# A hybrid encoder layer on one core: two single-half up-projection jobs instead of three, x split by token groups, and norm sums by a matrix of ones

## The chip, the cores and the metric

The kernel runs on one core of a Trainium2 chip. The metric is the device time of one execution in microseconds (us), shown as the median of several runs. TensorE (PE, with its weight loads PEld), VectorE (DVE), ScalarE (ACT), GpSimd (POOL) and the DMA queue of SyncE (SP) each work through a list of their own and wait for each other by semaphores.

## What is computed

One layer of an encoder trunk for 1024 prompt frames and 64 sample frames of width 1024. The two groups are laid side by side as 1088 columns (tokens) of eight tiles of 128 rows (features), and they share all weights. The reference, cut to its skeleton:

```python
mem_k, mem_v = rms_norm(mem) @ xk_w, rms_norm(mem) @ xv_w        # 256 memory tokens, prompt only
h = rms_norm(x, norm_mix_g)
q, fl, iv, og, ca, cg, pu = split(h @ w_in)
mix = [HGRN2(q, fl, iv, og), conv31(ca * sigmoid(cg)), pooling(pu)]
x = x + concat(mix) @ w_out
x = x + cross_attention(rms_norm(x, norm_x_g), mem_k, mem_v)      # 4 heads
h = rms_norm(x, norm_ffn_g)
x = x + square(relu(h @ w_up)) @ w_down                           # 1024 -> 4096 -> 1024
y = rms_norm(x, final_g)
```

rms_norm divides each token by the root of the mean of its squares over the 1024 features, and multiplies by a gain per feature. Besides y, the states, the caches and the memory keys and values are outputs.

## The kernel before

All operands of the large products are kept as a high and a low part (hi, lo; for weights wh, wl), each rounded to a format that TensorE takes at one column per step, and a product is three matmuls: hi by hi, lo by hi, hi by lo (`mm3`). The high part is a copy by ACT (`act`, line 126), the low part is what is left, by DVE (`split_lo`, line 138, or a scalar_tensor_tensor, line 141, where a gain is applied too). Weights arrive as raw blocks of 128x1024 (tile wr), `prep` (line 166) splits one into wh and wl; three split blocks fit in the pool, four raw ones. Working tiles come from a pool of 35 slots, results of products from 2 x 4 banks of 512 columns, tagged d (psd) and m (psm). Where the program does not fix the order by `inorder`, a scheduler places the instructions of each engine.

The stages, in order of time:

**Memory** (`memory`, line 290). Eight blocks of wk make the keys, and meanwhile x is loaded and its squares are summed. Then eight steps k (lines 362 to 378) multiply the memory by the blocks of wv: a step is 12 matmuls of 512 columns. After step 1 the norm of x is computed (`rstd_cols` and `bcast_rows`), and from step 2 on each step also issues, for one of the eight tiles of x, `scale_x` (x times the norm, DVE, 1088 columns) and `normed` (hi by ACT, then lo by DVE, which waits for hi). The last two tiles follow behind the loop.

**Mixers** (`mixers`, line 432). The input projection is 18 blocks of 128 columns, each a `dense` (line 212): three groups of tokens (364, 364, 360), and in each group eight tiles k by three matmuls. The first block goes across: for each k all three groups, so that it can begin when only the first tiles of x are split. Its four first blocks make the gated input of the convolution (csig, a sigmoid by ACT, and glu, a product by DVE). Later heads, convolution and pooling run beside the products.

**Attention** (line 785). The norm comes from `rstd_rows`: for nine tiles of 128 tokens a product of the squares (as the stationary operand) by one column of ones, then root (ACT) and reciprocal (DVE) on 9 columns, then a product with the identity for each of the nine tiles to spread the values over all rows, then copies by ACT into the tile rb.

**Up projection** (`mlp`, line 1109, and `up`, line 1061). It is a Strassen-like scheme: the tokens are cut into two halves c = 0 and 1 of 544, and each half gets seven operands "1" to "7" (th, tl), made by sums and splits of quarters (`operands`, line 967; its steps are called a for half 0, b for half 1). The 32 output blocks are 16 pairs; the weights of a pair are summed (`pair_sums`, 4 sums of 128x512) and split (`pair_units`, eight parts of 128x512). A job is one pair for one or for both halves: seven products in the order 1562734, each 12 matmuls of 272 columns and half. With LATE = 3 the jobs are: pairs 0 to 2 for half 0, pairs 3 to 15 for both halves, pairs 0 to 2 for half 1, 19 in all. In a job of one half the sums run on DVE, else on POOL. The steps of half 1 are spread over the first jobs by the lists handed to `up` (lines 1154 to 1157): its norm (rbb, from `rstd_half`, line 956), its operands (b), and at the end the loads and splits of the first results for the down projection (t_load, sp) and of the residual (xr_load).

**Down projection and end** (lines 1160 to 1227). Results are read back by blocks of four, split, multiplied and added to xr. The last block runs by three groups of tokens of 416, 416 and 256; behind each group its norm is computed (line 1206), POOL multiplies the first two groups by it, and DVE and POOL share the third.

Of the kernel before, what the change touches and what calls it, by code (L numbers as in the profile page):

```python
# [4 lines left out]
F32 = mybir.dt.float32  # L5
F32R = mybir.dt.float32r
U8 = mybir.dt.uint8
AF = mybir.ActivationFunctionType
# [3 lines left out]
P = 128  # L12
# [27 lines left out]
LATE = 3  # L40
# [12 lines left out]
class Trunk:  # L53
# [201 lines left out]
    def rstd_rows(self, sqs, dim, tag="m"):  # L255
        return self.bcast_rows(self.rstd_cols(sqs, TT, dim, tag), tag)

    def bcast_rows(self, r, tag="m"):
        rb = self.slot(n="rb")
        for (t0, m), tts, c0 in zip(SEGS, (TT[0:4], TT[4:8], TT[8:9]), (0, 4, 8)):  # L260
            ps = self.bank(tag)
            self.bcast_cols(ps, r, tts, t0, c0)
            self.act(rb[:, t0:t0 + m], ps[:, :m], AF.Copy)
        return rb
# [25 lines left out]
    def memory(self):  # L290
# [71 lines left out]
        for k in range(KT):  # L362
            wh, wl = self.weights()
            wh = wh.rearrange("p k n -> p (k n)")
            wl = wl.rearrange("p k n -> p (k n)")
            for m in range(2):
                for n in range(2):
                    sl = slice(512 * n, 512 * n + 512)
                    self.mm3_t(banks[m][n], xs[k][0][:, m * P:m * P + P], xs[k][1][:, m * P:m * P + P], wh[:, sl],
                               wl[:, sl], k == 0, k == KT - 1)  # L370
            if k == X_COLS:
                r_x = self.rstd_cols([accs[1]], TT, D, "d")
            elif k == X_ROWS:
                rx = self.bcast_rows(r_x, "d")
                self.act(self.warm, self.eps, AF.Sigmoid)
            if k >= X_ROWS:
                self.scale_x(k - X_ROWS, rx)
                hs.append(self.normed(k - X_ROWS))
# [5 lines left out]
        for j in range(KT - X_ROWS, KT):  # L384
            self.scale_x(j, rx)
            hs.append(self.normed(j))
# [16 lines left out]
    def scale_x(self, k, rb):  # L403
        x = self.xraw[k][:, :T]
        self.tt(x, x, rb[:, :T], MUL)

    def normed(self, k):
        x = self.xraw[k][:, :T]
        return self.hl(x, self.vec("mix_g", k))
# [22 lines left out]
    def mixers(self, xs):  # L432
# [10 lines left out]
        first = True  # L443

        glus = []
        for c in range(2):
            sig = self.slot(n="csig")
            self.dense(self.weights(), xs, ks, plain(sig, AF.Sigmoid), across=first)
            first = False
            glu = self.slot(n="glu")  # L450
            nc.gpsimd.memset(glu[:, 0:HIST], 0.0)
            nc.scalar.dma_start(glu[:, HIST + TP:2 * HIST + TP], a["cconv"][:, c, :])

            def ev(b, t0, m):
# [4 lines left out]
            self.dense(self.weights(), xs, ks, ev)  # L459
            nc.scalar.dma_start(a["o_convp"][c * P:c * P + P, :], glu[:, TP:TP + HIST])  # L460
            nc.scalar.dma_start(a["o_convs"][c * P:c * P + P, :], glu[:, HIST + T:HIST + T + HIST])
            glus.append(glu)
# [493 lines left out]
    def rstd_half(self, c):  # L956
        r = self.rstd_cols([self.accs[c]], CT, D, "m")
        yield
        for tts, c0 in ((CT[:4], 0), (CT[4:], 4)):
            ps = self.bank("m")  # L960
            t0, m = tts[0][0], sum(x[1] for x in tts)
            self.bcast_cols(ps, r, tts, t0, c0)
            self.act(self.rb[:, c, t0:t0 + m], ps[:, :m], AF.Copy)
        yield
# [144 lines left out]
    def mlp(self, o, x1, x2src):  # L1109
# [38 lines left out]
        def xr_load():  # L1148
# [7 lines left out]
            NPAIR: [lambda: t_load(f0)], NPAIR + 1: [sp, xr_load, sp, xr_load, sp, xr_load, sp],  # L1156
            NPAIR + 2: [xr_load] * 5})
# [32 lines left out]
        for g in ((0, 416), (416, 416), (832, 256)):  # L1190
# [14 lines left out]
            tts = [(c, min(P, m - c)) for c in range(0, m, P)]  # L1205
            r = self.rstd_cols([acc, sq] if last else [acc], tts, D)
            ps = self.bank("m")
            self.bcast_cols(ps, r, tts, 0)
            self.act(acc[:, :m], ps[:, :m], AF.Copy)
# [182 lines left out]
```

## Time and profile before

| what | value |
|---|---|
| time, median of 3 runs | 1566.14 us (1560.39 to 1567.87) |
| the profiled execution, its own time | 1564.72 us |
| its span, first to last instruction | 1562.9 us |
| DVE busy | 902.6 us (58%) |
| ACT busy | 587.5 us (38%) |
| POOL busy | 123.2 us (8%) |
| granted TensorE clock, mean | 0.993 |

Spans and stages below are of the profiled execution; times are counted from its first instruction. A busy time of PE contains modelled ends of pipelined matmuls that overlap; what PE really lost in a stretch is read from the number of matmuls in it (x...), against the number in an undisturbed stretch of the same length.

### The profile page before, as it was taken

What the parts mean: (1) busy time and instruction counts of PE and PEld (TensorE: products, weight loads), DVE (VectorE), ACT (ScalarE), POOL (GpSimd) and SP (SyncE); (2) the same over time, 40 slices, a digit from 0 to 9 for tenths busy, and PEclk for the clock granted to TensorE, in tenths of its full rate; (3) what the DMA queues carried; (4) which work ended last, traced back from release to release, by engine and by line L of the source; (5) the groups of instructions that cost most, each with busy time, mean ns of one, the idle gap of its engine ahead of it and who ended that gap; (6) DMA issues with size and microseconds to landing.
All of it is one profiled execution on the core that took longest, in us unless ns stands there. A gap on an engine that the chain in (4) does not pass through costs nothing.

```text
span 1562.9 us, 24283 instructions
## 1 busy us (share of the span) xinstructions
PE 1532.2 (98%) x10204; PEld 1486.5 (95%) x10204; DVE 902.6 (58%) x1329; ACT 587.5 (38%) x1072; POOL 123.2 (8%) x101
## 2 busy tenths in 40 slices
PE   8999999999999999999998999999999999999997
PEld 7799898999999999989998999999999999999997
DVE  7638988375654433684579545555585444434434
ACT  7422213556372222463555344444463111111133
POOL 0100001200000000000001222222100000000005
PEclk9999999999999999999999999999999999999999
DMA  9421011010013311223532233232286223211003
GB/s 347 137 83 55 15 41 32 18 41 18 31 66 145 127 55 55 68 78 113 184 113 97 98 112 112 98 112 85 98 320 241 99 100 109 94 59 53 29 1 115
DMA packets 54941, 150.58 MB, mean 96 GB/s; under 512 B 6704, under 2 KB 14384, under 8 KB 54832
## 3 DMA queue, kind: packets, MB, share of 16 engines
q1 hardware_dynamic: 51952, 148.37, 27.3%
q8 instruction: 80, 1.31, 0.3%
q10 hardware_dynamic: 2880, 0.66, 0.2%
q14 instruction: 29, 0.24, 0.0%
HBM read 115.11 MB, written 33.91 MB: 95 GB/s over the span
## 4 chain that ended last, share of the span: by engine, by line
PE 85%; issue 6%; DVE 4%; ACT 2%; POOL 1%; DMA 1%; SPq 0%; POOLq 0%; ACTq 0%; DVEq 0%
PE psd L210 66%; PE psm L210 13%; PE psm L560 3%; POOL xr L137 1%; DVE wl L138 1%; ACT hi L126 1%; PE psm L638 1%; DVE x L138 1%; PE psm L612 0%; PE psm L640 0%; PE psm L542 0%; DMA t<-tt 0%; PE psd L881 0%; DMA wr<-wk 0%; ACT L126 0%
## 5 line engine op out<-in xcount | busy, mean ns | idle before, releaser
L210 PE MATMUL psd<-hi,wl 128*128 128x364 f32 (+3 forms) x1536 | 507.0, 330 | 0.3 <-DVE wl L138 0.3
L210 PE MATMUL psd<-lo,wh 128*128 128x364 f32 (+3 forms) x1536 | 506.2, 330 | 0.9 <-DVE lo L141 0.9
L210 PE MATMUL psd<-hi,wh 128*128 128x364 f32 (+3 forms) x1536 | 505.4, 330 | 1.5 <-ACT hi L126 0.8
L126 ACT ACTIVATE wh<-wr 128x1024 fp32r<-128x1024 f32 (+1 forms) x178 | 160.5, 905 | 483.9 <-PE psd L210 342.8
L210 PEld LDWEIGHTS psd<-hi,wh 128*128 128x128 f32 x1536 | 288.8, 188 | 3.5 <-ACT hi L126 1.5
L210 PEld LDWEIGHTS psd<-lo,wh 128*128 128x128 f32 x1536 | 289.1, 188 | 2.2 <-DVE lo L141 1.5
L210 PEld LDWEIGHTS psd<-hi,wl 128*128 128x128 f32 x1536 | 289.0, 188 | 1.4 <-DVE wl L138 0.6
L138 DVE TENSOR_TENSOR wl<-wr,wh 128x1024 fp32r<-128x1024 f32 (+1 forms) x178 | 185.8, 1049 | 125.3 <-ACT wh L126 125.0
L138 DVE TENSOR_TENSOR xr<-psd,xr 128x364 f32<-128x364 f32 (+3 forms) x192 | 102.0, 533 | 177.4 <-PE psd L210 177.2
L210 PE MATMUL psd<-th,wh 128*128 128x272 f32 x448 | 130.6, 292 | 1.9 <-ACT wh L126 0.8
L210 PE MATMUL psm<-th,wh 128*128 128x272 f32 x448 | 130.4, 292 | 1.9 <-ACT wh L126 1.1
L210 PE MATMUL psd<-th,wl 128*128 128x272 f32 x448 | 129.7, 291 | 2.4 <-DVE wl L138 2.3
L210 PE MATMUL psd<-tl,wh 128*128 128x272 f32 x448 | 129.2, 289 | 0.0
L210 PE MATMUL psm<-th,wl 128*128 128x272 f32 x448 | 129.2, 290 | 0.0
L210 PE MATMUL psm<-tl,wh 128*128 128x272 f32 x448 | 129.1, 289 | 0.0
L210 PEld LDWEIGHTS psm<-th,wh 128*128 128x128 f32 x448 | 84.5, 189 | 3.4 <-ACT wh L126 1.5
L210 PEld LDWEIGHTS psd<-th,wh 128*128 128x128 f32 x448 | 84.6, 189 | 3.1 <-DVE t L138 1.1
L210 PEld LDWEIGHTS psd<-th,wl 128*128 128x128 f32 x448 | 84.4, 189 | 3.2 <-DVE wl L138 3.2
L210 PEld LDWEIGHTS psd<-tl,wh 128*128 128x128 f32 x448 | 84.7, 189 | 0.0
L210 PEld LDWEIGHTS psm<-tl,wh 128*128 128x128 f32 x448 | 84.7, 189 | 0.0
L210 PEld LDWEIGHTS psm<-th,wl 128*128 128x128 f32 x448 | 84.4, 189 | 0.0
L141 DVE SCALAR_TENSOR_TENSOR cacc<-glu,vecs,cacc 128x1118 f32<-128x1118 f32 x60 | 80.6, 1379 | 0.5
(249 smaller groups left out, 2375.0 us busy)
## 6 DMA issues: line engine op xcount, KB each, us to landing
wr<-w_up SPq DMA_DIRECT2D x38, 512.0 KB, 3.9
tt<-t SPq DMA_DIRECT2D x32, 544.0 KB, 3.1
t<-tt SPq DMA_DIRECT2D x32, 544.0 KB, 5.0
wr<-w_down SPq DMA_DIRECT2D x32, 512.0 KB, 3.3
wr<-w_in SPq DMA_DIRECT2D x18, 512.0 KB, 3.2
x<-res SPq DMA_DIRECT2D x16, 544.0 KB, 2.8
wr<-xo SPq DMA_DIRECT2D x16, 512.0 KB, 3.4
x<-xT SPq DMA_DIRECT2D x8, 544.0 KB, 8.3
```

Of the source, the lines that this page charges most:

```text
L126: return self.inorder("act", lambda: self.nc.scalar.activation(out, in_, f, **kw))
L137: return self.inorder("pool", lambda: eng.tensor_tensor(out, a, b, op))
L138: return self.inorder("dve", lambda: self.nc.vector.tensor_tensor(out, a, b, op))
L141: return self.inorder("dve", lambda: self.nc.vector.scalar_tensor_tensor(out, in0, s, in1, op0, op1))
L210: return self.inorder("pe", lambda: self.nc.tensor.matmul(*args, **kw))
L560: mm(pv[:m, c], k[:, c * P:c * P + m], qc[:, :, 1, :], start=True, stop=True)
L638: mm(ps[:w, c * P:c * P + P], sc[:w, s:s + w], vt[:w, s:s + P], start=True, stop=first)
```

## The change

There are four edits.

1. LATE goes from 3 to 2: pairs 0 and 1 alone are done half by half, pair 2 becomes the first job of both halves; 18 jobs. The side steps at the end move one job earlier: the load of the first results into the last job of both halves, their splits into the first single job of half 1.
2. x is split by pieces of one tile and one token group, group by group (24 pieces of 364 or 360 columns in place of 8 of 1088), two pieces behind each step of wv from step 2 on, the rest behind the loop. The low part of a piece is issued behind the scaling of the next piece.
3. The first three blocks of the input projection run group by group: group 0 for all three, then group 1, then group 2. They hold all three split weight blocks until then, and the next two are split behind them.
4. The norms of attention, of both halves and of the first two groups at the end come from one product per segment with a 128x128 matrix of ones as the stationary operand and the squares as the moving one. It gives the sum on all rows at once; ACT takes the root from the bank into the tile, DVE inverts the whole row in place. The norms of the memory, of x and of the last group at the end stay as they were.

```diff
-LATE = 3
+LATE = 2
...
-    def rstd_rows(self, sqs, dim, tag="m"):
-        return self.bcast_rows(self.rstd_cols(sqs, TT, dim, tag), tag)
...
+    def rstd_rows(self, sqs, dim, segs=SEGS, rb=None, tag="m"):
...
+        for t0, m in segs:
+            ps = self.bank(tag)
+            for i, sq in enumerate(sqs):
+                self.mm(ps[:, :m], self.ones, sq[:, t0:t0 + m], start=i == 0, stop=i == len(sqs) - 1)
+            r = rb[:, t0:t0 + m]
+            self.act(r, ps[:, :m], AF.Sqrt, scale=1.0 / dim, bias=self.eps)
+            self.inorder("dve", lambda: self.nc.vector.reciprocal(r, r))
         return rb
...
             if k >= X_ROWS:
-                self.scale_x(k - X_ROWS, rx)
-                hs.append(self.normed(k - X_ROWS))
+                for _ in range(2):
+                    next(steps)
...
+    def normed(self, hs, pieces, rb):
+        late = None
+        for k, (t0, m) in pieces:
+            if t0 == 0:
+                hs.append((self.slot(F32R, n="hi"), self.slot(F32R, n="lo")))
+            x, (hi, lo) = self.xraw[k][:, t0:t0 + m], (y[:, t0:t0 + m] for y in hs[k])
+            gain = self.vec("mix_g", k)
+            self.tt(x, x, rb[:, t0:t0 + m], MUL)
+            self.act(hi, x, AF.Copy, scale=gain)
+            if late:
+                self.stt(*late)
+            late = (lo, x, gain, hi.bitcast(F32), MUL, SUB)
+            yield
+        self.stt(*late)
...
+        for g in GROUPS:
+            for w, ev in zip(ws, evs):
+                self.dense(w, xs, ks, ev, groups=[g])
+        for _ in range(2):
+            self.prep()
+        self.dense(self.weights(), xs, ks, evs[3])
...
     def rstd_half(self, c):
-        r = self.rstd_cols([self.accs[c]], CT, D, "m")
-        yield
-        for tts, c0 in ((CT[:4], 0), (CT[4:], 4)):
-            ps = self.bank("m")
-            t0, m = tts[0][0], sum(x[1] for x in tts)
-            self.bcast_cols(ps, r, tts, t0, c0)
-            self.act(self.rb[:, c, t0:t0 + m], ps[:, :m], AF.Copy)
-        yield
+        for seg in ((0, 512), (512, H - 512)):
+            self.rstd_rows([self.accs[c]], D, [seg], self.rb[:, c])
+            yield
...
-            NPAIR: [lambda: t_load(f0)], NPAIR + 1: [sp, xr_load, sp, xr_load, sp, xr_load, sp],
-            NPAIR + 2: [xr_load] * 5})
+            NPAIR - 1: [lambda: None] * 4 + [lambda: t_load(f0)], NPAIR: [sp, xr_load, sp, xr_load, sp, xr_load, sp],
+            NPAIR + 1: [xr_load] * 5})
...
+            else:
+                acc = self.rstd_rows([acc], D, [(0, m)])
```

In the lists of instructions below, a row is the line, the operation, out<-in with the numbers of the tiles, and the shape; the numbers differ between the two kernels.

On DVE, in the loop over wv, steps k = 2 to 4: before, each step is a scaling, a low part and the low part of a weight block (wl).

```order
L138 TENSOR_TENSOR x_105<-x_105,rb_541 128x1088
L141 SCALAR_TENSOR_TENSOR lo_560<-x_105,vecs,hi_559 128x1088
L138 TENSOR_TENSOR wl_564<-wr_474,wh_563 128x1024
L138 TENSOR_TENSOR x_126<-x_126,rb_541 128x1088
L141 SCALAR_TENSOR_TENSOR lo_583<-x_126,vecs,hi_582 128x1088
L138 TENSOR_TENSOR wl_587<-wr_493,wh_586 128x1024
```

The same place in the changed kernel, with the step behind it:

```order
L138 TENSOR_TENSOR x_165<-x_165,rb_541 128x364
L141 SCALAR_TENSOR_TENSOR lo_586<-x_148,vecs,hi_585 128x364
L138 TENSOR_TENSOR wl_596<-wr_493,wh_595 128x1024
L138 TENSOR_TENSOR x_203<-x_203,rb_541 128x364
L141 SCALAR_TENSOR_TENSOR lo_591<-x_165,vecs,hi_590 128x364
L138 TENSOR_TENSOR x_238<-x_238,rb_541 128x364
L141 SCALAR_TENSOR_TENSOR lo_614<-x_203,vecs,hi_613 128x364
L138 TENSOR_TENSOR wl_624<-wr_527,wh_623 128x1024
```

Between two wl now stand two scalings and two low parts of a third of the length, and each low part stands behind the scaling of the next piece (lo_591 is of x_165, and the scaling of x_203 stands between them).

On DVE, at the start of the up projection (sq and acc are the squares of half 1, t the results of job 0, df and tl the operands of half 1): before,

```order
L138 TENSOR_TENSOR tl_7197<-res_6634,th_7196 128x544
L247 RECIPROCAL rc_7223<-rc_7223 128x4
L247 RECIPROCAL rc_7223<-rc_7223 32x1
L138 TENSOR_TENSOR df_7250<-res_6563 128x544
L138 TENSOR_TENSOR df_7250<-res_6634 128x544
L138 TENSOR_TENSOR wl_7298<-wr_6864,wh_7297 128x512
L138 TENSOR_TENSOR tl_7254<-df_7250,th_7253 128x1088
```

and in the changed kernel:

```order
L138 TENSOR_TENSOR tl_7215<-res_6664,th_7214 128x544
L138 TENSOR_TENSOR df_7261<-res_6593 128x544
L273 RECIPROCAL masks<-masks 128x512
L138 TENSOR_TENSOR df_7261<-res_6664 128x544
L273 RECIPROCAL masks<-masks 128x32
L138 TENSOR_TENSOR t_7220<-psd_7289,t_7220 128x272
L138 TENSOR_TENSOR wl_7304<-wr_6882,wh_7303 128x512
L138 TENSOR_TENSOR tl_7265<-df_7261,th_7264 128x1088
```

The two small reciprocals became one of 512 columns and one of 32, in the tile masks that holds the norms of both halves, and they stand ahead of the weights and operands of the coming jobs.

On DVE, at the start of the third token group at the end (facc and fsq are the squares of the final norm): before,

```order
L138 TENSOR_TENSOR xr_10774<-psd_14061,xr_10774 128x256
L247 RECIPROCAL rc_14033<-rc_14033 128x3
L247 RECIPROCAL rc_14033<-rc_14033 32x1
L138 TENSOR_TENSOR xr_10817<-psd_14077,xr_10817 128x256
L138 TENSOR_TENSOR facc_14060<-facc_14060,fsq_14091 128x256
```

and in the changed kernel:

```order
L138 TENSOR_TENSOR xr_10753<-psd_14018,xr_10753 128x256
L273 RECIPROCAL rb_13996<-rb_13996 128x416
L138 TENSOR_TENSOR xr_10796<-psd_14034,xr_10796 128x256
L138 TENSOR_TENSOR xr_10839<-psd_14052,xr_10839 128x256
L138 TENSOR_TENSOR xr_10876<-psd_14070,xr_10876 128x256
L138 TENSOR_TENSOR facc_14017<-facc_14017,fsq_14048 128x256
```

The norm of the second group is now a reciprocal of 416 columns, and the additions of the third group are placed later behind it.

More of the change, by code (lines that the diff above doesn't have):

```diff
@@ L263, in bcast_rows @@
             self.act(rb[:, t0:t0 + m], ps[:, :m], AF.Copy)
+        return rb
+    def rstd_rows(self, sqs, dim, segs=SEGS, rb=None, tag="m"):
+        if rb is None:
+            rb = self.slot(n="rb")
+        for t0, m in segs:
[5 more added lines that the diff above has]
+            self.inorder("dve", lambda: self.nc.vector.reciprocal(r, r))
         return rb
@@ L375, in memory @@
                 self.act(self.warm, self.eps, AF.Sigmoid)
+                pieces = [(j, g) for g in GROUPS for j in range(KT)]
+                steps = self.normed(hs, pieces, rx)
             if k >= X_ROWS:
-                self.scale_x(k - X_ROWS, rx)
-                hs.append(self.normed(k - X_ROWS))
+                for _ in range(2):
+                    next(steps)
         for m in range(2):
@@ L383, in memory @@
             self.behind.append(lambda m=m, vo=vo: (a["o_memv"][m * P:m * P + P, :], vo[:, :1024]))
-        for j in range(KT - X_ROWS, KT):
-            self.scale_x(j, rx)
-            hs.append(self.normed(j))
+        for _ in steps:
+            pass
         self.expand_masks()
@@ L401, in sq_two @@
         self.tt(acc, acc, sq[:, :T], ADD)
[L403 to L409, printed above, removed]
+    def normed(self, hs, pieces, rb):
[12 more added lines that the diff above has]
+        self.stt(*late)
     def mm3_t(self, out, xh, xl, wh, wl, first, last):
@@ L441, in plain @@
             return ev
-        first = True
-        glus = []
+        while len(self.wq) < 3:
+            self.prep()
+        ws, self.wq = self.wq, []
+        sigs, glus, evs = [], [], []
         for c in range(2):
-            sig = self.slot(n="csig")
-            self.dense(self.weights(), xs, ks, plain(sig, AF.Sigmoid), across=first)
-            first = False
+            sigs.append(self.slot(n="csig"))
             glu = self.slot(n="glu")
@@ L452, in mixers, with ev @@
             nc.scalar.dma_start(glu[:, HIST + TP:2 * HIST + TP], a["cconv"][:, c, :])
-            def ev(b, t0, m):
+            glus.append(glu)
+            def ev(b, t0, m, glu=glu, sig=sigs[c]):
                 e = min(m, TP - t0)
@@ L458, in ev @@
                     self.tt(glu[:, 2 * HIST + t0 + e:2 * HIST + t0 + m], b[:, e:m], sig[:, t0 + e:t0 + m], MUL)
-            self.dense(self.weights(), xs, ks, ev)
+            evs += [plain(sigs[c], AF.Sigmoid), ev]
+        for g in GROUPS:
+            for w, ev in zip(ws, evs):
+                self.dense(w, xs, ks, ev, groups=[g])
+        for _ in range(2):
+            self.prep()
+        self.dense(self.weights(), xs, ks, evs[3])
+        for c, glu in enumerate(glus):
             nc.scalar.dma_start(a["o_convp"][c * P:c * P + P, :], glu[:, TP:TP + HIST])
             nc.scalar.dma_start(a["o_convs"][c * P:c * P + P, :], glu[:, HIST + T:HIST + T + HIST])
-            glus.append(glu)
         self.bg.append(self.chain(self.conv(glus, mix), 2))
@@ L1204, in mlp @@
                     self.act(v, v, AF.Copy, scale=self.vec("final_g", o))
[L1205 to L1209, printed above, removed]
+            if last:
+                tts = [(c, P) for c in range(0, m, P)]
+                r = self.rstd_cols([acc, sq], tts, D)
+                ps = self.bank("m")
+                self.bcast_cols(ps, r, tts, 0)
+                self.act(acc[:, :m], ps[:, :m], AF.Copy)
+            else:
+                acc = self.rstd_rows([acc], D, [(0, m)])
             if not last:
```

## The prediction

> **What bounds the kernel now.** I read the page first (how busy is PE), then a table of stretches (where does PE lose time), then the timeline of those stretches (what is it waiting for). The first two lines of the page:
>
> ```profile
> span 1562.9 us, 24283 instructions
> ...
> PE 1532.2 (98%) x10204; PEld 1486.5 (95%) x10204; DVE 902.6 (58%) x1329; ACT 587.5 (38%) x1072; POOL 123.2 (8%) x101
> ```
>
> PE is the bound nearly everywhere, so there are two ways to win: matmuls that go away, and stretches in which PE waits. In the table of stretches the columns are length, then busy time and count of PE, PEld, DVE, ACT, POOL, then the granted clock, the DMA share and GB/s:
>
> ```profile
> 50.00:68.00 18.00, 16.00 (x61) 12.15 (x61) 12.36 (x10) 9.54 (x11) 0.00 (x0) 0.91 0.23 80
> 58.10:61.50 3.40, 1.75 (x7) 0.92 (x6) 3.26 (x3) 1.05 (x2) 0.00 (x0) 1.00 0.08 30
> 61.50:64.90 3.40, 3.40 (x10) 2.65 (x9) 2.13 (x3) 2.15 (x2) 0.00 (x0) 0.50 0.45 154
> 68.00:88.00 20.00, 17.30 (x96) 15.31 (x95) 14.97 (x12) 10.25 (x13) 1.01 (x1) 1.00 0.39 139
> 88.00:108.00 20.00, 20.00 (x122) 20.00 (x121) 4.13 (x6) 4.02 (x7) 0.00 (x0) 1.00 0.18 56
> 269.70:276.60 6.90, 6.45 (x26) 6.30 (x27) 2.35 (x5) 0.00 (x0) 0.00 (x0) 0.51 0.00 0
> 812.00:866.00 54.00, 49.10 (x358) 46.63 (x357) 46.30 (x66) 31.97 (x58) 5.27 (x3) 0.97 0.33 110
> 820.00:861.00 41.00, 36.10 (x264) 33.95 (x264) 39.87 (x55) 24.55 (x43) 5.27 (x3) 0.99 0.27 92
> 880.00:920.00 40.00, 40.00 (x320) 40.00 (x319) 20.52 (x28) 15.76 (x31) 11.12 (x8) 1.00 0.32 109
> 1131.00:1167.00 36.00, 34.65 (x264) 33.43 (x263) 30.72 (x44) 23.66 (x40) 0.00 (x0) 1.00 0.80 287
> ```
>
> Undisturbed, the input projection runs 122 matmuls in 20 us (0.164 us each) and the up projection 320 in 40 us (0.125 us). By that, 68 to 88 us lacks 20 - 96 x 0.164 = 4.3 us. From 812 to 866 us, the three single jobs at the start, 54 - 358 x 0.125 leaves about 9 us lost (a little less, since a few records are missing). The single jobs at the end lose at most 36 - 264 x 0.125 = 3 us. So the stretches that the change touches hold some 20 us of waiting. The clock belongs to it: in the 3.4 us from 58.1 PE was half idle, and in the next 3.4 us it was granted half the clock, which costs 1.7 us.
>
> Why PE waits around 60 us, in the loop over wv, stands in the timelines of PE and of DVE (start, length, and in brackets the idle time before it and who ended it):
>
> ```profile
> 58.01 0.39 PE L210 MATMUL psm<-wl,mhi 128*128 128x512 f32 x1
> 58.24 0.39 PE L210 MATMUL psm<-wh,mlo 128*128 128x512 f32 x1
> 59.20 0.50 PE L210 MATMUL psm<-wh,mhi 128*128 128x512 f32 x1 [0.58 <-ACT wh L126]
> 60.78 0.50 PE L210 MATMUL psm<-wl,mhi 128*128 128x512 f32 x1 [1.08 <-DVE wl L138]
> ```
>
> ```profile
> 54.55 1.22 DVE L138 TENSOR_TENSOR wl<-wr,wh 128x1024 fp32r<-128x1024 f32 x1
> 55.68 1.28 DVE L138 TENSOR_TENSOR x<-x,rb 128x1088 f32<-128x1088 f32 x1
> 58.24 1.35 DVE L141 SCALAR_TENSOR_TENSOR lo<-x,vecs,hi 128x1088 fp32r<-128x1088 f32 x1 [1.28 <-ACT hi L126]
> 59.51 1.22 DVE L138 TENSOR_TENSOR wl<-wr,wh 128x1024 fp32r<-128x1024 f32 x1
> ```
>
> DVE makes one wl every 59.51 - 54.55 = 4.96 us, of which 1.28 us are a wait for ACT's hi of the same tile; a step of PE is 12 matmuls 0.227 us apart (512 columns, 58.01 to 58.24), 2.7 us. PE starves for weights. 61 x 0.227 = 13.9 us, so 50 to 68 us lacks 4.1 us, and together with the stretch behind it 8.4 us are lost here.
>
> **Edits 2 and 3: x in pieces, the first three blocks by groups.** A step of DVE becomes two scalings, two low parts and a wl, with no wait for ACT, since another scaling stands between. For a DVE operation of 364 columns on these tiles there is no row; I scale the tile's cost by columns and add a start. The 1088-column scaling takes 1.28 us and the low part 1.27 us from start to start (timeline above); a third of these plus 0.06 us of start gives 0.49 and 0.48, or 0.97 for a piece. The step is then 2 x 0.97 + 1.13 = 3.1 us in place of 4.96, still a little over PE's 2.7, so over the three steps left some 0.35 us each, 1 us in all, stay lost. Behind the loop PE needs only group 0, whose eight pieces are done by step 5; the 12 pieces left take DVE 11.6 us, while PE has three blocks by 24 matmuls by 0.164 = 11.8 us for each group. So the 4.3 us from 68 to 88 go, and with both stretches dense the half clock at 61.5 goes too. Gain 8.4 - 1.0 = **7.4 us**. The lower bound is 4: the pieces cost 0.15 us more each (24 x 0.15 = 3.6 us of DVE), and DVE stays the bound. The upper bound is 8.4. What could be late next is a bank: the product of block 2 by group 0 is read by DVE behind all 24 pieces, and the bank is wanted again at the sixth product, 5 x 3.94 = 19.7 us behind the start; 11.6 us of pieces and two wl fit in that. The fourth weight block is split while PE is in the second and third block of group 2 (7.9 us against about 2.3 us for ACT and DVE).
>
> **Edit 4: sums by ones.** What PE spends now on the norm of attention, and what DVE does then:
>
> ```profile
> 551.49 2.15 PE L210 MATMUL psm<-ones,acc 128*128 128x1 f32 x18
> ...
> 555.00 2.31 PE L210 MATMUL psm<-ident,rc 128*128 128x128 f32 x18
> ```
>
> ```profile
> 553.98 0.30 DVE L247 RECIPROCAL rc<-rc 128x8 f32<-128x8 f32 x2 [1.28 <-ACT rc L126]
> 563.75 1.51 DVE L141 SCALAR_TENSOR_TENSOR qf<-psd,rb 128x364 f32<-128x364 f32 x3 [9.47 <-PE psd L210]
> ```
>
> The new product is a plain float32 matmul of up to 512 columns, and reciprocals of whole rows. The nearest rows are the pooling's matmul and the small reciprocals (count, then busy us and mean ns of one):
>
> ```profile
> L761 PE MATMUL psm<-ws,poolw 128*128 128x512 f32 x8 | 3.8, 593 | 0.0
> ...
> L868 DVE RECIPROCAL mx<-mx 128x2 f32<-128x2 f32 x16 | 2.6, 160 | 1.7 <-ACT pr L126 1.3
> ...
> L247 DVE RECIPROCAL rc<-rc 128x8 f32<-128x8 f32 x2 | 0.4, 203 | 2.8 <-ACT rc L126 2.8
> ```
>
> The pooling issues four products of 512 columns and the row has 8 records in 3.8 us: 0.95 us each. 1088 columns are 2.0 us, 544 are 1.0, 416 are 0.77. A reciprocal grows from 160 to 203 ns with 6 columns more, 7.2 ns a column: 3.8 us for 512, 8.1 us for the 1088 of attention, 3.1 us for 416. The bounds are far apart, because no row has more than 8 columns: from 1.1 ns a column, the price of the scaling (1.22 us for 1024), to 14 ns, twice the slope; I take the slope. [...]
>
> Attention: PE gives up 4.46 us and takes 2.0, **2.5 us** gained. The reciprocals are 8.1 us, and DVE was idle 9.47 us before its first use of rb; its last row is there in time, if only just. If not hidden at all they would cost 8 us. The first half's norm falls into the output projection, where PE is dense and DVE has gaps: ten products and ten spreads at about 0.12 us (2.15 and 2.31 over 18) are 2.4 us, against 1.0: **1.3 us**, the last 32 columns counted with a start. The end:
>
> ```profile
> 1541.04 0.98 PE L210 MATMUL psm<-ones,facc 128*128 128x1 f32 x8
> 1542.65 1.20 PE L210 MATMUL psm<-ident,rc 128*128 128x128 f32 x8
> ```
>
> ```profile
> 1544.48 9.54 POOL L137 TENSOR_TENSOR xr<-xr,facc 128x416 f32<-128x416 f32 x8 [10.22 <-ACT facc L126]
> 1556.71 2.09 POOL L137 TENSOR_TENSOR y<-xr,facc 128x256 f32<-128x256 f32 x3 [2.69 <-ACT facc L126]
> ```
>
> Each of the two groups saves PE 2.18 - 0.77 = 1.4 us, 2.8 in all. But the second group's norm comes later, by the 3.1 us of the reciprocal against two small ones, a spread and a copy: root and reciprocal end near 1545.6 where POOL began at 1544.48. POOL has 2.69 us to spare before the last group's work, so about 1.1 + 1.4 of it is used, and the third group's additions on DVE start behind the reciprocal. I take **2 us** of the 2.8 (bounds 2.8 and -1).
>
> **Edits 1 and 4 at the start of the up projection.** From 820 to 861 us DVE is busy 39.87 of 41 us: there it is the bound, not PE, and the 9 us lost are its backlog. How the norm of half 1 sits in it:
>
> ```profile
> 816.88 0.29 DVE L247 RECIPROCAL rc<-rc 128x4 f32<-128x4 f32 x2 [0.32 <-ACT rc L126]
> 817.10 1.33 DVE L138 TENSOR_TENSOR df<-res 128x544 f32<-128x544 f32 x2
> 819.22 0.69 DVE L138 TENSOR_TENSOR wl<-wr,wh 128x512 fp32r<-128x512 f32 x1 [0.79 <-ACT wh L126]
> 820.50 1.29 DVE L138 TENSOR_TENSOR tl<-df,th 128x1088 fp32r<-128x1088 f32 x1 [0.59 <-ACT th L126]
> ```
>
> 544 columns at 7.2 ns are 3.9 us, less 0.3 for the small ones and 0.8 + 0.6 of idle time that it fills: everything behind it, the weights of job 1 first, is 2.2 us late, and PE, which is 1.4 us earlier, waits. Against that stands one single job less: its weights are 8 splits and 4 sums of 512 columns at 0.69 us (the wl row just above), 8.2 us of DVE, and job 2 now has 21 us of PE work to cover the last two operands of half 1. Most of that relief comes behind the waits of job 1 though, which has the heaviest load (three operand steps). The bounds: a gain of 8.2 - 2.2 = 6 us, and a loss of 2.2 + 1.7 for one more stretch at half clock. I take a gain of **2 us**, nearer to the middle, with one such stretch in it: 3 us of waiting within 3.4 us is more than the half-idle stretch from 58.1 that led to one. [...]
>
> At the end of the up projection one of three single jobs goes, with up to a third of the 3 us; the splits of the first results (four of 1.3 us on DVE) now meet the first single job instead of the second. **1 us** (bounds 2 and -1). The two weight loads that go, 512 KB each, are waited for by nobody.
>
> **The sum.** 7.4 + 2.5 + 1.3 + 2 + 2 + 1 = 16.2 us. The profiled execution took 1564.7 us, its span 1562.9 and 1.8 around it; minus 16.2 gives 1548.5. The median of the runs was 1566.14, 1.4 above that execution, so I predict 1549.5 us for the median. What can shift it without being a cost of the change: the 6.9 us at half clock from 269.7, behind a wait in the mixers, cost 3.4 us and may last one stretch less, or one more may come.
>
> **The rivals.**
>
> - *DVE stays the bound at the start of the up projection, and edit 1 brings nothing.* The reciprocal delays job 1, the load of job 1 stays, and POOL's sums now run in job 2 beside the last operands. The term goes from +2 to -4: 1555.5 us. For it: DVE is full there. Against: job 2 doubles PE's work per weight.
> - *The pieces do not free DVE.* The shift may not be enough, since ACT also has the wh in its row, and three blocks by groups hold all split weights. Then 2 of the 7.4 us are left: 1555 us. For it: DVE would still need 3.1 us for a step of 2.7. Against: the wait of 1.28 us per step has its cause in one tile, and that is cut.
> - *Both of these*: 1561 us.
> - *Slower: a row's reciprocal costs far more than the slope of the small ones.* Places: attention (1088 columns, hidden up to 9.5 us plus 2.5 saved), the start of the up projection (544, not hidden), the end (416). At 24 ns a column attention lacks 26 - 12 = 14 us, the up projection 13 - 4 = 9 us more, the end 10 - 3 = 7 us more, in all 30 us on top: 1579.5 us. It makes the change slower than no change from about 17 ns. For it: no row shows a long one. Against: 2, 3, 4 and 8 columns lie on one line.
> - *The change does not do what it says*, for edit 1: the same matmuls stay, and only work of DVE, POOL and DMA goes; that is the first rival.
>
> **How the numbers follow.** About 0.5%, 7.8 us, is what a measurement here can tell from no change. My forecast, 1543 to 1553 us, gets 0.60; a better case (the half clocks stay away, 6 us at the up projection, near 1541) 0.04; the first rival 0.14; the second 0.14; both 0.04; the slow one 0.04. Range 1541 to 1560: it takes in the single rivals, and leaves out half of the case of both, the slow one and the tails. Faster by over 0.5% means below 1558.3: the forecast, the better case and most of the single rivals, 0.83; same 0.13; slower 0.04.
>
> **What would show it.** In the changed profile: 122 matmuls in nearly every 20 us from 65 to 125; wl in the wv loop every 3.0 to 3.3 us with no wait on ACT; psm<-ones with 512 columns, two records of 0.43 us; reciprocals of 128x512 of 3.5 to 4.5 us; the first qf of attention not behind a reciprocal; a PE wait of 2 to 4 us at the start of job 1, then none worth a us until the jobs of both halves run evenly. I would be wrong if the reciprocal costs over 10 ns a column, if PE still lacks over 4 us from 50 to 88, or if the start of the up projection loses more than the 9 us of now.

## The result and the profile after

The changed kernel takes **1547.3 us** in the median of 5 runs (1546.6 to 1549.0), the kernel before 1565.4 in the same comparison: a ratio of 0.9891, with a 95% interval of 0.9876 to 0.9905. Forecast were 1549.5 us and a range of 1541 to 1560. In a second comparison, beside the experiments, the changed kernel took 1548.3 and the kernel before 1562.7 (0.9908, 0.9895 to 0.9921). By the medians the gain is 18.1 us in the one and 14.4 in the other; the two intervals together allow 12 to 19. The profiled execution took 1546.6 us against 1564.7 before. The first lines of its page:

```profile
span 1544.5 us, 24124 instructions
...
PE 1518.3 (98%) x10114; PEld 1474.8 (95%) x10114; DVE 916.6 (59%) x1347; ACT 587.2 (38%) x1073; POOL 138.2 (9%) x105
```

PE is busy 13.9 us less, the span is 18.4 shorter. The table of stretches, cut at the same places of the program (columns as in the prediction):

```profile
50.00:68.00 18.00, 15.46 (x66) 11.60 (x66) 12.78 (x21) 9.61 (x16) 0.00 (x0) 1.00 0.30 94
68.00:88.00 20.00, 20.00 (x122) 20.00 (x121) 17.62 (x34) 13.81 (x24) 1.01 (x1) 1.00 0.37 128
263.50:270.30 6.80, 6.45 (x26) 6.30 (x27) 2.25 (x5) 0.00 (x0) 0.00 (x0) 0.50 0.00 0
700.40:703.80 3.40, 3.40 (x13) 2.74 (x12) 1.60 (x3) 1.39 (x3) 0.00 (x0) 0.50 0.00 0
803.00:857.00 54.00, 51.53 (x394) 49.77 (x392) 51.57 (x67) 33.42 (x59) 19.49 (x7) 1.00 0.30 101
1114.00:1150.00 36.00, 35.31 (x274) 34.52 (x272) 28.44 (x40) 21.89 (x36) 1.29 (x1) 1.00 0.68 253
```

From 68 us on the input projection is dense (122 matmuls in 20 us); before, 96 stood there. The first 54 us of the up projection hold 394 matmuls in place of 358, although DVE is still full (51.57 of 54 us). The clock is not at half at 61.5 any more, nor at 44.5 and 860.2, where the profile before has it too (0.51 and 0.54 granted there, 1.00 at all three places now); it still is in the mixers (263.5), and it now is at 700.4.

Where the time came from is best read stage by stage. The stages are cut in the trace at the start of the first matmul of each; times in us. The columns are the kernel before and the changed one, the three parts of the change each alone, and the changed kernel with the old norms (edits 1 to 3); each is one profiled execution.

| stage | before | changed | edit 1 | edits 2+3 | edit 4 | 1 to 3 |
|---|---|---|---|---|---|---|
| wv loop to the values' product | 108.4 | 102.1 | 106.9 | 102.1 | 108.4 | 103.5 |
| values to the norm of attention | 407.0 | 407.0 | 405.4 | 407.2 | 407.1 | 407.0 |
| norm and queries of attention | 96.7 | 94.2 | 98.3 | 98.3 | 94.2 | 98.3 |
| scores and values of attention | 65.3 | 66.2 | 66.3 | 66.2 | 66.3 | 66.3 |
| output projection, with half 0's norm | 99.1 | 97.7 | 99.1 | 99.1 | 97.7 | 99.1 |
| up projection | 353.7 | 346.2 | 345.2 | 351.1 | 356.9 | 345.2 |
| down projection | 334.4 | 334.0 | 334.0 | 334.4 | 334.4 | 334.0 |
| last block, with the norms of the end | 55.2 | 53.8 | 55.2 | 55.2 | 54.0 | 55.2 |

Between the two kernels these are 6.3 us at the front, 2.5 in attention, -0.9 behind it, 1.4, 7.5 in the up projection, 0.3 and 1.4. The -0.9 is the stretch at half clock at 700.4: without one, the changed kernel's second profile takes 65.3 us there, as before.

### The profile page after: what moved, and what is told of

Read it like the earlier page. It is cut to its first block, busy times and chain, and to the rows that moved or that the text cites. A ratio compares the mean times of both kernels' runs of the same rounds, so it can differ in the third digit from the quotient of the medians.

```text
span 1544.5 us, 24124 instructions
## 1 busy us (share of the span) xinstructions
PE 1518.3 (98%) x10114; PEld 1474.8 (95%) x10114; DVE 916.6 (59%) x1347; ACT 587.2 (38%) x1073; POOL 138.2 (9%) x105
## 4 chain that ended last, share of the span: by engine, by line
PE 93%; DVE 3%; ACT 2%; issue 1%; POOL 1%; DMA 0%; SPq 0%; POOLq 0%; ACTq 0%
PE psd L210 73%; PE psm L210 13%; PE psm L587 3%; DVE wl L138 1%; ACT wh L126 1%; POOL xr L137 1%; PE psm L665 1%; PE psd L908 1%; PE psm L639 1%; PE psm L667 0%; PE psm L569 0%; DMA wr<-wk 0%; PE psm L677 0%; PE psm L604 0%; PE psm L788 0%
```

## The experiments

The medians stand beside the kernel before of the same comparison (1562.5 for the first four rows, 1562.7 for the next four, 1563.7 for the last two). In each expectation "theory A" and "rival" are two readings set against each other before the run; "ones" is short for the norms by a matrix of ones.

| kernel | us | ratio, 95% interval |
|---|---|---|
| edit 1 alone | 1556.4 | 0.9962 (0.9949 to 0.9975) |
| edit 4 alone | 1561.4 | 0.9989 (0.9978 to 0.9999) |
| edits 2 and 3 alone | 1560.1 | 0.9985 (0.9976 to 0.9994) |
| changed, wh between the pieces | 1545.5 | 0.9890 (0.9876 to 0.9905) |
| changed, again | 1548.3 | 0.9908 (0.9895 to 0.9921) |
| wh between, old norm of half 1 | 1543.9 | 0.9879 (0.9865 to 0.9894) |
| changed, all norms old | 1551.7 | 0.9931 (0.9918 to 0.9944) |
| changed, reciprocals three times | 1573.2 | one run |
| changed, no groups | 1553.2 | 0.9933 (0.9918 to 0.9948) |
| wh between, old norm of half 1 and of the second group of the end | 1542.3 | 0.9871 (0.9854 to 0.9887) |

**The changed kernel, again.**

> The changed kernel, unaltered, to stand beside the others on the same chip: 1547 us, and 15 to 18 us faster than the kernel before.

It came in at 14.4 us, just under the expected 15 to 18; the stages agree with the first profile within 0.9 us, but for 1.6 more at the front (a stretch at half clock, below).

**Edit 1 alone.**

```
-LATE = 3
+LATE = 2
...
-            NPAIR: [lambda: t_load(f0)], NPAIR + 1: [sp, xr_load, sp, xr_load, sp, xr_load, sp],
-            NPAIR + 2: [xr_load] * 5})
+            NPAIR - 1: [lambda: None] * 4 + [lambda: t_load(f0)], NPAIR: [sp, xr_load, sp, xr_load, sp, xr_load, sp],
+            NPAIR + 1: [xr_load] * 5})
```

> The kernel before with edit 1 alone (two single jobs, side steps one job earlier); the norms, x and the first blocks stay as before. In the profile before, the first two single jobs lose 2.7 and 2.2 us (half 1's norm included), the third 2.5 and the first half of the first double job 4.3. Theory A: what was lost in the third and behind it is the backlog of one single job too many on DVE, and it goes with that job, whatever the norms do; job 0 and 1 keep their losses, the end gains 0.9. That is 6.5 to 7.7 us faster than the kernel before (about 1558). Rival (the prediction's term, +2 at the start and +1 at the end, edit 1 with edit 4): the relief comes too late for most of the backlog, and the gain alone is 3 us or less (1562 or more).

6.1 us faster by the medians, 8.5 by the stage. The 6.5 to 7.7 of theory A lie between the two, and the rival's 3 us or less are out (the interval is 3.9 to 8.0 us). The mechanism of theory A is seen in the start of the up projection, here in blocks of 84 products of the operands (one single job, or half a job of both halves; 10.59 us when nothing waits):

| kernel | block 1 | 2 | 3 | 4 |
|---|---|---|---|---|
| before | 13.33 | 12.77 | 13.07 | 14.94 |
| edits 2+3 alone (old norms, three jobs) | 13.33 | 12.79 | 13.04 | 12.34 |
| edit 4 alone (ones, three jobs) | 13.39 | 13.99 | 13.57 | 16.27 |
| edit 1 alone (old norms, two jobs) | 13.33 | 12.02 | 10.57 | 10.59 |
| changed (ones, two jobs) | 13.39 | 12.96 | 10.58 | 10.59 |

The loss in blocks 3 and 4 goes whole with the third single job. (Block 4 of the kernel before holds a stretch at half clock and a wait longer by 1.1 us; edits 2 and 3 alone, with the same code there, have neither, so 2.6 of the 8.5 us may be of that execution alone.) PE's waits there, in the timeline of PE before, from block 3 on:

```profile
845.86 0.39 PE L210 MATMUL psd<-th,wh 128*128 128x272 f32 x1 [0.46 <-ACT t L126]
850.32 0.39 PE L210 MATMUL psm<-th,wh 128*128 128x272 f32 x1 [0.57 <-ACT wh L126]
853.78 0.39 PE L210 MATMUL psd<-th,wl 128*128 128x272 f32 x1 [0.57 <-DVE wl L138]
858.69 0.39 PE L210 MATMUL psd<-th,wl 128*128 128x272 f32 x1 [1.74 <-DVE wl L138]
```

All but the first end at weights, the two in the job of both halves at DVE's low parts: DVE had not caught up when that job began. In the timeline of PE after, two waits of over 0.1 us are left in the whole start, both in the single jobs:

```profile
815.32 0.39 PE L210 MATMUL psd<-th,wh 128*128 128x272 f32 x1 [1.28 <-DVE t L138]
828.25 0.39 PE L210 MATMUL psd<-th,wh 128*128 128x272 f32 x1 [1.09 <-ACT wh L126]
```

**Edit 4 alone.** In the kernel before only `rstd_rows`, `rstd_half` and the norms of the end are those of the changed kernel.

```
+                self.mm(ps[:, :m], self.ones, sq[:, t0:t0 + m], start=i == 0, stop=i == len(sqs) - 1)
...
+            self.inorder("dve", lambda: self.nc.vector.reciprocal(r, r))
```

> The kernel before with edit 4 alone (norm sums by a matrix of ones). Theory A: 2.4 us gained in attention, 1.3 at the first half's norm, 1.4 at the end, and the reciprocal of half 1 costs nothing or little at the start of the up projection, since its two pieces fall into DVE's idle time: 4 to 5.5 us faster (about 1560.5). Rival (the prediction): with three single jobs behind it the reciprocal makes the start of the up projection 2.2 us later, and up to 1.7 more by a stretch at half clock: 1 to 3 us faster.

1.1 us faster by the medians (interval 0.2 to 3.4): the rival, the prediction's own reading for three jobs, is right, and theory A's 4 to 5.5 are out. Attention, half 0 and the end gain 2.5, 1.4 and 1.2 us; the up projection gives 3.3 back against the kernel before, 5.9 against edits 2 and 3 alone. Some 3.0 of the 5.9 us are two stretches at half clock, at 836 and 860. This profile is of the longest of the twelve executions (1564.3 us, 3.0 above the median), so in most of them the loss was probably smaller. What stands in front of PE, in DVE's timeline of the changed kernel (edit 4 alone has the same order and the same wait of 1.28 us):

```profile
807.16 0.72 DVE L138 TENSOR_TENSOR df<-res 128x544 f32<-128x544 f32 x1
807.91 3.35 DVE L273 RECIPROCAL masks<-masks 128x512 f32<-128x512 f32 x1
811.18 0.66 DVE L138 TENSOR_TENSOR df<-res 128x544 f32<-128x544 f32 x1
811.76 0.34 DVE L273 RECIPROCAL masks<-masks 128x32 f32<-128x32 f32 x1
812.02 0.38 DVE L138 TENSOR_TENSOR t<-psd,t 128x272 f32<-128x272 f32 x1
...
814.83 0.43 DVE L138 TENSOR_TENSOR t<-psd,t 128x272 f32<-128x272 f32 x1
```

The second t here is what PE waits for at 815.32: not a weight but a bank, which DVE reads late behind the reciprocal.

**Edits 2 and 3 alone.**

```
+                pieces = [(j, g) for g in GROUPS for j in range(KT)]
+                steps = self.normed(hs, pieces, rx)
...
+        for g in GROUPS:
+            for w, ev in zip(ws, evs):
+                self.dense(w, xs, ks, ev, groups=[g])
```

> The kernel before with edits 2 and 3 alone (x in pieces, first three blocks by groups). Theory A: the step from wl to wl is 4.25 us as in the changed kernel, PE loses about 4 us from 50 to 70 and none behind it: 4.6 us faster without the stretch at half clock from 44.5, 6.3 with it gone too. Rival (the prediction): 7.4 us. The start of the up projection loses as much as before (11.7 us).

The front takes 102.1 us as in the changed kernel, 6.3 less than before, and the step of DVE is 4.25 us; the profiled executions differ by 5.3 us. But the medians differ by 2.3 us only (interval 0.9 to 3.8), so neither the 4.6 to 6.3 of theory A nor the rival's 7.4 came in the time. The start of the up projection lost 9.2 us, not 11.7. In this profile attention holds a stretch at half clock near 550 (1.6 us) and one near 706 (1.0), which the profile before lacks; on the other hand the kernel before is 2.3 us faster in the median here than its own profiled execution.

**ACT's wh between the two pieces.**

```
             if k >= X_ROWS:
-                for _ in range(2):
-                    next(steps)
+                next(steps)
+                wl_part = self.prep_hi() if k < KT - 1 else None
+                next(steps)
+                if wl_part:
+                    wl_part()
```

> The changed kernel, with ACT's copy of the next weight block (wh) issued between the two pieces of a step instead of behind both, and its wl behind them. Theory A: in the changed kernel wl waits 1.1 us a step for wh, because ACT has it behind the second hi, which waits for DVE's second scaling; with wh ahead of that hi the step falls from 4.25 to about 3.1 us, PE loses about 1 us in place of 4 up to 70 us: 2.5 to 3 us faster than the changed kernel (about 1544.5). Rival: the step is bound by the sum of DVE and ACT work (ACT 1.1 + 2 x 0.5 us, DVE 3.1) and by the weights' arrival; the step stays above 3.9 us and the time within 1 us of the changed kernel.

The wait that theory A named is shown. DVE's timeline of the loop, first in the changed kernel, then here:

```profile
56.74 1.23 DVE L138 TENSOR_TENSOR wl<-wr,wh 128x1024 fp32r<-128x1024 f32 x1 [1.11 <-ACT wh L126]
57.88 0.53 DVE L138 TENSOR_TENSOR x<-x,rb 128x364 f32<-128x364 f32 x1
58.33 0.59 DVE L141 SCALAR_TENSOR_TENSOR lo<-x,vecs,hi 128x364 fp32r<-128x364 f32 x1
58.84 0.53 DVE L138 TENSOR_TENSOR x<-x,rb 128x364 f32<-128x364 f32 x1
59.29 0.59 DVE L141 SCALAR_TENSOR_TENSOR lo<-x,vecs,hi 128x364 fp32r<-128x364 f32 x1
60.98 1.22 DVE L138 TENSOR_TENSOR wl<-wr,wh 128x1024 fp32r<-128x1024 f32 x1 [1.11 <-ACT wh L126]
```

```profile
56.03 1.23 DVE L138 TENSOR_TENSOR wl<-wr,wh 128x1024 fp32r<-128x1024 f32 x1 [0.15 <-ACT wh L126]
...
59.32 1.23 DVE L138 TENSOR_TENSOR wl<-wr,wh 128x1024 fp32r<-128x1024 f32 x1 [0.15 <-ACT wh L126]
```

A step falls from 4.24 to 3.29 us (3.1 expected). The reason stands in ACT's timeline of the changed kernel:

```profile
58.45 0.60 ACT L126 ACTIVATE hi<-x,vecs 128x364 fp32r<-128x364 f32 x1 [1.74 <-DVE x L138]
59.40 0.60 ACT L126 ACTIVATE hi<-x,vecs 128x364 fp32r<-128x364 f32 x1 [0.36 <-DVE x L138]
59.91 1.04 ACT L126 ACTIVATE wh<-wr 128x1024 fp32r<-128x1024 f32 x1
```

The copy wh needs nothing from DVE, but it is queued behind the second hi, which waits for DVE's second scaling; then DVE waits for wh. Each of the two engines waits once a round for the other. With wh ahead of that hi the front takes 98.8 us, 3.4 less than in the changed kernel. The whole time does not settle the size: this kernel is 17.0 us under the kernel before, the changed one 18.1 and 14.4.

**Old norm of half 1 in that kernel.** `rstd_half` takes the old form for c = 1 only.

```
+        if c == 0:
+            yield from self.rstd_ones(c)
+            return
+        r = self.rstd_cols([self.accs[c]], CT, D, "m")
```

> The kernel with wh between the pieces, and in it the norm of half 1 alone by the old form (products with one column, small reciprocals, spread by the identity). Theory A: with edit 1 alone the first two single jobs took 13.33 and 12.02 us, in the changed kernel 13.39 and 12.96; the row reciprocals (3.35 and 0.34 us) on a full DVE cost the 0.9 us more in the second job, and the old form gives them back: 1.0 us faster than wh between the pieces, 3.4 faster than the changed kernel (1544). Rival: the order of the operand steps and POOL's sums make job 1 slow, not the reciprocal; job 1 stays at 12.9 us and the time at 1545.

Theory A: the second block takes 12.02 us again (12.96 with ones), the up projection 345.2 in place of 346.2. The whole, wh and norm together, is 4.4 us faster than the changed kernel in the same comparison, and no run of the one reaches into those of the other.

**All norms old, the rest changed.** `rstd_rows`, `rstd_half` and the norms of the end are those of the kernel before.

> The changed kernel with all norms in the old form (edits 1 to 3 without edit 4). Theory A: edit 4 is worth more here than alone (1.1 us by the medians), since with two single jobs the reciprocal of half 1 costs 0.9 us and not 3.3; attention loses 2.4 us (3.9 if the stretch at half clock at 550 comes, as in both kernels with the old norm and edits of the front or of the jobs), the first half 1.4, the end 1.4, the start of the up projection gains 0.9: 4.3 to 6 us slower than the changed kernel. Rival: edit 4 is worth what it was worth alone, 1 us.

3.4 us slower than the changed kernel by the medians. By the stages it is 4.1 in attention, 1.4 at half 0 and 0.8 to 1.4 at the end, less 1.0 in the up projection: 5.3 to 5.9, as theory A had it; 1.6 of the 4.1 are a stretch at half clock at 550. By the medians edit 4 is worth three times what it was worth alone, but less than the expected 4.3, and with the interval of 0.2 to 3.4 of edit 4 alone the medians can't part the two values for certain; the stages do.

**Each row reciprocal three times.**

```
+            for _ in range(3):
                 self.inorder("dve", lambda: self.nc.vector.reciprocal(r, r))
```

> The changed kernel with each row reciprocal done three times in place (the value stays the same), so 2 x 6.97 us more on DVE in attention, 2 x 3.7 at each half, 2 x 2.7 at each of the two groups of the end. Theory A, stage by stage: attention has banks for PE to go on, four products of 4 us from 547.1, so PE stalls from 563 until the first bank is read at 568.5: 5.5 us lost. Half 0 lies in gaps of DVE: 0 to 1. Half 1 meets a full DVE: 6 to 7.4 lost in jobs 0 to 2. The end: 5 us, since the second group's POOL work and the third group's additions stand behind. In all 17 to 19 us more. Rival of the prediction: the cover in attention is only what DVE idled, 0.8 us are left of it, and 13 us are lost there (25 in all).

25 us more, as much as the rival said, but not in its places. Stage by stage against the changed kernel: attention 9.8, half 0 nothing (97.7), up projection 7.6, end 7.2; another 1.6 came in the scores, where the clock stayed at half for longer. In the up projection the wait for the bank that DVE reads behind the reciprocal grows from 1.28 to 8.10 us, so it is the reciprocal that makes it:

```profile
834.35 0.57 PE L210 MATMUL psd<-th,wh 128*128 128x272 f32 x1 [8.10 <-DVE t L138]
```

In attention, DVE's group of reciprocals, PE's wait, and the clock:

```profile
547.83 19.82 DVE L274 RECIPROCAL rb<-rb 128x512 f32<-128x512 f32 x7 [0.68 <-ACT rb L126]
```

```profile
568.10 0.67 PE L210 MATMUL psd<-hi,wh 128*128 128x364 f32 x1 [7.50 <-DVE qf L141]
```

```profile
562.00:564.90 2.90, 0.00 (x0) 0.00 (x0) 2.90 (x2) 0.00 (x0) 0.00 (x0) 1.00 0.00 0
564.90:568.30 3.40, 0.20 (x1) 0.20 (x2) 3.40 (x4) 0.00 (x0) 0.00 (x0) 0.62 0.00 0
568.30:572.00 3.70, 3.70 (x13) 3.70 (x14) 2.56 (x5) 1.10 (x1) 0.00 (x0) 0.50 0.16 27
```

PE stopped near 560.4, when its fourth bank was full, and waited 7.5 us; 2.2 us more went at half clock when it had work again. Theory A had put the end of the fourth bank at 563, 2.6 us too late, and left the clock out.

**Edit 3 undone.**

```
-        for g in GROUPS:
-            for w, ev in zip(ws, evs):
-                self.dense(w, xs, ks, ev, groups=[g])
+        for w, ev in zip(ws, evs):
+            self.dense(w, xs, ks, ev)
```

> The changed kernel with edit 3 undone: the first three blocks of the input projection one after the other, each with its three groups, while x is still split by pieces, group by group. In the changed kernel DVE ends the low part of the last piece of group 1 at 79.0 us and of group 2 at 86.7. Theory A: the first block then waits for these pieces, ends at about 87.3 in place of 77.1, and all behind it is 10 us late: 8 to 10 us slower than the changed kernel (1557). So it is the order by groups that covers the 12 pieces left. Rival: the pieces alone free DVE, and the groups only spread the waiting; less than 3 us slower.

4 to 8 us slower than the changed kernel by the medians (10.5 us under the kernel before, against 14.4 and 18.1), 3 to 5 between the profiled executions; the front takes 108.0 us, 5.9 more. The groups are needed, but theory A was too dark, as PE's timeline shows:

```profile
81.01 0.32 PE L210 MATMUL psd<-hi,wl 128*128 128x364 f32 x1
81.17 0.33 PE L210 MATMUL psd<-lo,wh 128*128 128x360 f32 x1
81.34 0.33 PE L210 MATMUL psd<-hi,wl 128*128 128x360 f32 x1
81.51 0.49 PE L210 MATMUL psd<-hi,wh 128*128 128x364 f32 x2
```

360 columns are group 2, 364 can only be a later block's: while the first block waits for pieces of group 2, the scheduler has put products of the next block between. The loss is that of group 1 (5.6 us: its 24 products, 4.0 us of work, last from 70.5 to 80.1), with a stretch at half clock in it.

**The second norm of the end in the old form.**

```
-            if last:
-                tts = [(c, P) for c in range(0, m, P)]
-                r = self.rstd_cols([acc, sq], tts, D)
+            if t0:
+                tts = [(c, min(P, m - c)) for c in range(0, m, P)]
+                r = self.rstd_cols([acc, sq] if last else [acc], tts, D)
```

> The best kernel so far (wh between the pieces, old norm of half 1), and in it the norm of the second group of the end by the old form too, the first group still by ones. Theory A: in the changed kernel the last group's additions stand behind the second row reciprocal (2.7 us) on DVE, and PE waits 1.7 us for facc; with the old form that wait goes to under 0.5, PE works 1.4 us more, so the time stays within 0.5 us of 1543.9, and the end was worth 1.4 in place of 2 for this wait. Rival: the wait for facc comes from POOL's work beside DVE (additions of 0.4 us take 1.1), not from the reciprocal; then the wait stays and the time is 1.4 us longer.

PE's products for the norms, first in the changed kernel, then here:

```profile
1522.37 0.97 PE L210 MATMUL psm<-facc,ones 128*128 128x416 f32 x2
1534.50 0.38 PE L210 MATMUL psm<-ones,facc 128*128 128x1 f32 x2 [1.58 <-DVE facc L138]
```

```profile
1518.41 0.98 PE L222 MATMUL psm<-ones,facc 128*128 128x1 f32 x8
1520.02 1.20 PE L222 MATMUL psm<-ident,rc 128*128 128x128 f32 x8
1530.53 0.38 PE L222 MATMUL psm<-ones,facc 128*128 128x1 f32 x2
```

The wait of 1.58 us for facc is gone, PE works 1.2 us more, and the last block takes 53.9 us against 53.5 in the kernel without this edit. Theory A holds. The median lies 1.6 us below that kernel's, but in another comparison, and the intervals overlap: no difference. These two are the fastest versions run.

## Why the prediction was right, and where not

The total was right (16.2 us forecast, 18.1 between the profiled executions, 14 to 18 between medians), and partly by luck, because two sizes missed in opposite directions.

*The step of 3.1 us in the wv loop failed.* It said: with no wait for ACT, since another scaling stands between. The wait for hi did go, but a wait of 1.11 us for ACT's wh took its place, and the step became 4.25 us. I had counted DVE's work and not the order of ACT's queue. PE loses 3.1 us in the loop (its last five steps take 16.7 us from 48.57, in place of 5 x 2.72) and 1.0 in the first block: 4.1 against the 1 forecast, just over the mark that the prediction itself had set for being wrong. The second rival was nearer in its reason (ACT also has wh in its row) than in its price (2 us left of the term). The term of 7.4 us measures 4.7 when kernels of like clock are compared (108.4 to 103.7 for the changed kernel's second profile, both with a stretch at half clock at 44.5; 106.9 for edit 1 alone to 102.1, both without): inside its bounds, near the lower. The 6.3 us of the first profile hold 1.6 of that stretch, which this profile happened not to have. The rest of the edit did what was said, in kind: pieces of 0.96 us against 0.97 forecast (the 0.06 us of start in it was given without a row; DVE's rows of 544 and 272 columns at 849.36 and 850.00 in the profile before last 0.64 and 0.35 us from start to start, and 2 x 0.35 - 0.64 is 0.06), and a dense projection behind 70 us. With wh moved, the front gains 8.1 us without that stretch, near the upper bound of 8.4.

*The half clock at 61.5 was mispriced.* The prediction gave it 1.7 us of its own. Edit 1 alone, with the old code there, has no half clock at 61.5 and longer waits for weights instead (0.58 and 1.07 us, where the kernel before waits 0.34 behind its slow stretch). From the first step that waits (at 59.20 in the kernel before) to the first product of the projection both take 9.9 us. PE had to wait for the weights anyway, so the slower clock cost nothing there.

*The start of the up projection was mis-sized the other way.* The prediction weighed a relief that comes behind the waits of job 1 against a reciprocal that delays it by 2.2 us, took +2, and put the end at +1. Measured: 7.5 us for the whole up projection against the kernel before, 4.9 against the profile with the same code there and no stretch at half clock at 860. The reciprocal costs 1.0 us of that, not 2.2 (in block 1 the 1.4 us that PE's shorter norm saves go into the wait for the bank, in block 2 0.9 are lost), and the half clock in the term did not come. Where the prediction put one wait of 2 to 4 us, at the start of job 1, there are two, 1.28 us for a bank in job 0 and 1.09 for weights in job 1. The relief was the larger part: I had priced the job's 8.2 us of DVE, but not looked where the 9 us were lost. Of the 11.7 us that the table of blocks shows before (54.1 - 4 x 10.59), 6.8 lay in the third job and the first half of the one behind it, and those are the ones that went. The end of the up projection gained 0.9 us (its last two blocks take 23.2 in place of 24.1), as forecast. The first rival (DVE stays bound, edit 1 brings nothing) is refuted by edit 1 alone, although its condition holds: DVE is full (51.57 of 54 us). But from the first job of both halves on, PE does not wait for that work: it runs 254 matmuls in the 32 us from 829.

*Edit 4.* Attention gained 2.5 us, as forecast. PE's products with the ones take 2.15 us for 1088 columns (the group from 545.16), 2.0 ns a column; the rounded parts, of which it was said that they go at one column per step, measure 0.44 to 0.46 ns a column (0.227 us for 512, 0.164 for 364 or 360, 0.125 for 272). The reciprocals cost these:

```profile
547.04 6.97 DVE L273 RECIPROCAL rb<-rb 128x512 f32<-128x512 f32 x3 [0.68 <-ACT rb L126]
554.85 1.52 DVE L141 SCALAR_TENSOR_TENSOR qf<-psd,rb 128x364 f32<-128x364 f32 x3 [0.83 <-PE psd L210]
```

6.97 us for 1088 columns are 6.4 ns a column against 7.2 forecast. (The lower bound of 1.1 ns a column was misread: the 1.22 us for 1024 columns are those of the low part of the weights, 1.2 ns a column. Nothing rests on it.) qf still waits for PE, 0.83 us, so they are hidden; the cover is larger than that, since PE can fill a fourth bank first: in the run with three reciprocals 12.9 us more on DVE ahead of the first qf (19.82 - 6.97) gave 7.5 us of waiting, so 5.4 were covered. The slow rival fell with the price. Half 0 gained 1.4 us (forecast 1.3), the end 1.4 in the first profile and 0.8 in the second (forecast 2): the additions behind the second reciprocal cost PE the 1.6 us that the last experiment takes away.

*The parts don't add up one by one.* By the medians they sum to 9.5 us alone, to 14 to 18 together. One interaction is shown: the ones cost 3.3 to 5.9 us in the up projection with three single jobs (some 3 of the 5.9 at half clock), and 1.0 with two. My reading, not tested by itself, is that the backlog runs on into the next job only when that has little work for PE. The rest I can't place: stretches at half clock come and go between executions, 0.9 to 1.6 us each by the stages, and the medians of the kernel before differ by 3 us between comparisons.

## What to carry to other kernels

A wait that is cut can show the next one in the queue of the other engine (here 1.28 us a step for hi became 1.11 us for wh, and the step went from 4.24 to 3.29 us when wh was moved): when two engines feed each other, write down the order of both, and put the instruction that waits for nobody ahead of the one that does. Where an engine is full, look in which block the bound engine loses time, not how much work is full: removing work helps the blocks behind it, and the same reciprocal weighed 1 us with two single jobs and some 3 to 6 with three. Try edits that touch the same backlog together, too.

## What was not expected of the hardware

The clock was granted at half also where PE shows no gap. In attention with the old norm (edit 1 alone), the 18 products of one column stand in the first of these two stretches, and the second is at half:

```profile
547.40:550.80 3.40, 3.40 (x26) 3.13 (x25) 2.73 (x3) 1.11 (x2) 0.00 (x0) 1.00 0.74 257
550.80:554.20 3.40, 3.40 (x14) 3.38 (x14) 0.30 (x2) 0.41 (x2) 0.00 (x0) 0.51 0.00 0
```

```profile
548.92 2.20 PE L210 MATMUL psm<-ones,acc 128*128 128x1 f32 x18
```

Such a stretch came there in 3 of 4 profiles with one-column products and in none of the 7 with the matrix of ones and a single reciprocal; it cost 1.6 us (98.3 against 96.7). The norm of x, which has such products in all kernels, was followed by one at 44.5 in 4 of 12 profiles. Once, in the kernel before, the 18 products stood in one such stretch (550.9 to 554.3) and the clock stayed full (1.00 there and in the next 3.4 us). With three reciprocals the half clock came in a wait of 7.5 us (0.62 granted from 564.9, 0.50 from 568.3), so PE stood idle ahead of it; ahead of the stretch above it did not. What brings it there no run shows.

POOL's first sum of the up projection took 8.64 us in the changed kernel, 1.41 before, and DVE's low parts of 1024 columns took up to 2.30 us while POOL was adding, 1.22 else. (A POOL span is rough.) Since PE was dense there (254 matmuls in the 32 us from 829), nothing of it showed in the time.
